# Hybrid encoder on 8 cores: two of three groups of a 31-tap depthwise convolution moved from TensorE to VectorE, and LayerNorm row sums folded before the matmul with ones

## The chip, the cores and the metric

One Trainium2 chip, 8 cores, one program on all of them; each core computes 2048 of 16384 tokens (plus a halo of up to 60 on each side), with no exchange between cores. The metric is the device time of the slowest core, in microseconds. Executions come in two states: in the slow one, the cores of a die show a lower granted TensorE clock and the time is longer (one run of the kernel before: 0.82 on one die and 0.99 on the other, 6155 us against 5217 for a fast run).

In the profiled run of the kernel before TensorE does the 33720 matmuls, VectorE (DVE, 4501 instructions) and ScalarE (ACT, 2473) the elementwise work, and GpSimd (POOL) issues the weight loads and builds 744 small diagonal matrices. The kernel keeps its tiles in a memory called SBUF; its matmuls write to the tile `bank` in PSUM.

## The reference, cut to what matters

```python
for l in range(DEPTH):                                   # DEPTH = 4, D_MODEL = 1024
    x = layer_norm(ALPHA * x + 0.5 * swiglu_ffn(x, ...ffn1...), ...)
    x = layer_norm(ALPHA * x + hybrid_mixer(x, ...), ...)
    x = layer_norm(ALPHA * x + 0.5 * swiglu_ffn(x, ...ffn2...), ...)

# in hybrid_mixer: head group C (384 channels), beside a pooling group and a short gated convolution
a = c_val * jax.nn.sigmoid(c_gate)
a = depthwise_conv(a, cconv_w) + cconv_b                 # 31 taps, one filter per channel
y_c = jax.nn.silu(layer_norm(a, cnorm_g, cnorm_b))
```

## The kernel before

Channels lie on the 128 partitions, tokens along the free dimension, so 384 channels are three groups. Each core treats its tokens in two halves; the FFN of one half runs beside the mixer of the other. A small scheduler in Python emits all instructions at build time: it estimates durations, picks what is ready and so fixes the order of every engine. **Each engine then gets its list in this fixed order**, with waits on semaphores; below, a trace shows VectorE idle for 6.1 us at an instruction that has to wait, with work behind it in its list.

The convolution is done on TensorE: for each tap POOL multiplies the identity by the tap's weights, and TensorE multiplies the shifted data by that diagonal:

```python
def diags():                                             # POOL
    for c in range(3):
        for kk in range(31):
            yield Need("pool", [], [(dgp, 1)])           # one of 4 buffers
            b = dgp.get()
            v = view2("dg", dg_t, 2, b[1], P, 0, P)
            ev = ts(v, ident_v, vcol(V_CCONV + kk * 3 + c, li), 0.0, ALU.mult, ALU.add, eng="pool")
            # ... cut ...
for c in range(3):                                       # TensorE
    for kk in range(31):
        # ... cut: wait for the diagonal ...
        for ti, (c0, n) in enumerate(tb):                # three token tiles of some 350
            me = mm_part(bk[ti][1], n, [(dv, abuf(c, c0 - base + kk - 15, n))], kk == 0, kk == 30)
        dgp.put(b, me)
    # ... cut: ACT takes the three banks out with scale 0.5 and the bias ...
```

The LayerNorm over 1024 channels sums over partitions with a matmul by a tile of ones, for each of the 8 channel chunks, once for x and once for its square:

```python
for h in range(2):                                       # two halves of 4 chunks
    # ... cut ...
    e1 = copy(cast, XS3(4 * h, 4, c0, n), rate=2.0)      # DVE, fp32 to bf16
    e2 = act(sq, XS3(4 * h, 4, c0, n), AF.Square)        # ACT
    mm_part(banks[0][1], n, [(ones_v, row_of(cast, c, n)) for c in range(4)], h == 0, h == 1)
    pe_ev = mm_part(banks[1][1], n, [(ones_v, row_of(sq, c, n)) for c in range(4)], h == 0, h == 1)
```

## Time and profile before

| | kernel before |
|---|---|
| time, three runs | 5224, 5776, 6056 us (the first in the fast state) |
| later fast runs | mostly 5217 to 5228 us |
| span of the profiled run | 5217.6 us, fast |
| TensorE busy | 5066 us, 97% |
| DVE, ACT, POOL busy | 50%, 26%, 20% |
| the chain that ended last | 95% TensorE |

One reads such a page from the chain: what lies on it is what a change can shorten. Then from the group rows: a row gives line, engine, operation, what is written from what, count, busy time, mean of one, then the engine's idle time just before these instructions and what ended it. The lines themselves stand in the prediction below.

### The profile page before, as it was taken

The page shows a single profiled execution, that of the slowest core. Times are in us where ns is not written, and L with a number is a line of the kernel's source. Part 1 is how long each engine was busy: PE and PEld are TensorE (multiplying, and loading weights), DVE is VectorE, ACT ScalarE, POOL GpSimd, SP SyncE. Part 2 cuts the span into 40 slices and gives each one's busy share as a digit, 9 for nine tenths or more (in the row PEclk, how much of TensorE's full clock was granted, in tenths as well). Part 3 has the DMA queues.
Part 4 walks back from the last instruction along what each step waited for, and adds up shares of the span by engine and source line. Part 5 has one row for each costly group of instructions (what it writes and reads, how often), then busy time and mean ns, then how long its engine had stood idle before and what let it go on. Part 6 is the DMA issues. An engine that isn't in the chain of part 4 may idle for free.

```text
span 5217.6 us, 86568 instructions; the slowest of 8 cores (5204.5 to 5217.6 us)
## 1 busy us (share of the span) xinstructions
PE 5066.0 (97%) x33720; PEld 3278.2 (63%) x33720; DVE 2634.1 (50%) x4501; ACT 1366.4 (26%) x2473; POOL 1032.9 (20%) x2050
## 2 busy tenths in 40 slices
PE   5999999999999999999999999999999999999986
PEld 2665666666666666666666666666666666666654
DVE  0354654653535555555353555655535447447534
ACT  0132232221314124122121422422212133233212
POOL 1114114111111411411111221221111141141110
PEclk8999999999999999999999999999999999999998
DMA  8543553556655355355555435435455534434663
GB/s 149 70 67 45 71 68 47 69 68 74 71 72 69 45 70 68 48 71 72 73 71 73 61 53 74 62 53 74 71 74 73 72 48 72 71 48 63 79 90 73
DMA packets 206165, 357.56 MB, mean 69 GB/s; under 512 B 21072, under 2 KB 73552, under 8 KB 205776
## 3 DMA queue, kind: packets, MB, share of 16 engines
q0 software_dynamic: 192864, 334.30, 47.9%
q1 hardware_dynamic: 12912, 17.73, 1.5%
q8 instruction: 286, 4.69, 0.4%
q14 instruction: 103, 0.84, 0.1%
HBM read 677.78 MB, written 8.39 MB: 132 GB/s over the span
## 4 chain that ended last, share of the span: by engine, by line
PE 95%; DMA 2%; POOL 1%; issue 1%; DVE 1%; ACT 0%; ACTq 0%; POOLq 0%
PE bank L460 86%; PE bank L468 9%; DMA ringF<-wgu 1%; POOL dg L510 1%; DMA xb<-xin 1%; DMA ringF<-wd 0%; DVE xs L497 0%; DVE HM L503 0%; ACT HM L490 0%; ACT xs L490 0%; DVE nw L497 0%; DVE nw L503 0%; POOL ringF L523 0%; POOL ringM L523 0%; POOL xb L523 0%
## 5 line engine op out<-in xcount | busy, mean ns | idle before, releaser
L460 PE MATMUL bank<-xb,ringF 128*128 128x352 bf16 (+7 forms) x16896 | 2560.5, 312 | 73.7 <-DMA ringF<-wgu 60.7
L460 PEld LDWEIGHTS bank<-xb,ringF 128*128 128x128 bf16 x16896 | 1642.1, 97 | 963.0 <-issue 85.8
L460 PE MATMUL bank<-HF,ringF 128*128 128x352 bf16 (+7 forms) x8448 | 1282.0, 312 | 4.0 <-DMA ringF<-wd 4.0
L503 DVE SCALAR_TENSOR_TENSOR HF<-sgF,bank 128x352 bf16<-128x352 f32 (+7 forms) x1056 | 548.4, 519 | 1389.8 <-PE bank L460 1388.4
L490 ACT ACTIVATE sgF<-bank 128x352 f32<-128x352 f32 (+7 forms) x1056 | 489.4, 463 | 2469.0 <-PE bank L460 2463.1
L460 PEld LDWEIGHTS bank<-HF,ringF 128*128 128x128 bf16 x8448 | 823.0, 97 | 442.9 <-issue 4.3
L523 POOL DMA_DIRECT2D ringF<-wgu x704 | 383.1, 544 | 2418.6 <-PE bank L460 2407.4
L460 PE MATMUL bank<-xb,ringM 128*128 128x352 bf16 (+6 forms) x3264 | 498.2, 312 | 0.0
L497 DVE TENSOR_TENSOR xs<-xs,bank 128x352 f32<-128x352 f32 (+7 forms) x624 | 324.6, 520 | 325.0 <-PE bank L460 324.9
L497 DVE TENSOR_TENSOR xs<-xs,HM 128x1408 f32<-128x1408 f32 (+7 forms) x288 | 461.8, 1611 | 0.0
L460 PEld LDWEIGHTS bank<-xb,ringM 128*128 128x128 bf16 x3264 | 316.4, 97 | 172.1 <-issue 0.2
L523 POOL DMA_DIRECT2D ringF<-wd x384 | 203.3, 529 | 998.9 <-PE bank L460 989.1
L468 PE MATMUL bank<-HM,dg 128*128 128x352 bf16 (+6 forms) x2232 | 357.5, 318 | 33.7 <-POOL dg L510 33.7
L503 DVE SCALAR_TENSOR_TENSOR xs<-xs,agb,bank 128x352 f32<-128x352 f32 (+3 forms) x336 | 192.8, 577 | 317.9 <-PE bank L460 316.3
L510 POOL TENSOR_SCALAR dg<-identf,vecs 128x128 bf16<-128x128 f32 x744 | 326.4, 442 | 57.8 <-PE bank L468 14.5
L490 ACT ACTIVATE xb<-xs,vecs 128x352 bf16<-128x352 f32 (+7 forms) x528 | 328.3, 669 | 5.8 <-DVE xs L497 5.8
L468 PEld LDWEIGHTS bank<-HM,dg 128*128 128x128 bf16 x2232 | 216.3, 99 | 172.1 <-issue 57.5
L490 ACT ACTIVATE HM<-xs 128x1408 bf16<-128x1408 f32 (+4 forms) x144 | 192.2, 1366 | 475.7 <-DVE xs L497 274.8
L503 DVE SCALAR_TENSOR_TENSOR xs<-bank,agb,xs 128x352 f32<-128x352 f32 (+3 forms) x336 | 195.4, 582 | 153.1 <-PE bank L460 153.1
L460 PE MATMUL bank<-Y,ringM 128*128 128x352 bf16 (+5 forms) x1584 | 240.8, 311 | 0.0
L460 PEld LDWEIGHTS bank<-Y,ringM 128*128 128x128 bf16 x1584 | 154.7, 98 | 79.7
L468 PE MATMUL bank<-HM,ones 128*128 128x352 bf16 (+7 forms) x1152 | 192.2, 312 | 3.3 <-DVE HM L514 1.9
(47 smaller groups left out, 1727.6 us busy)
## 6 DMA issues: line engine op xcount, KB each, us to landing
ringF<-wgu POOLq DMA_DIRECT2D x704, 256.0 KB, 5.2
ringF<-wd POOLq DMA_DIRECT2D x256, 224.0 KB, 4.1
ringM<-win POOLq DMA_DIRECT2D x136, 256.0 KB, 4.5
ringF<-wd POOLq DMA_DIRECT2D x128, 256.0 KB, 4.6
ringM<-wout POOLq DMA_DIRECT2D x64, 256.0 KB, 4.4
xs<-xin SPq DMA_DIRECT2D x3, 1488.0 KB, 29.9
out<-xs SPq DMA_DIRECT2D x3, 1408.0 KB, 5.7
xs<-xin SPq DMA_DIRECT2D x2, 1400.0 KB, 41.8
```

Of the source, the lines that this page charges most:

```text
L460: ins = e.matmul(banks_t[b][:, :n], l.ap, r.ap, start=(i == 0), stop=(i == len(prs) - 1))
L468: ins = e.matmul(banks_t[b][:, :n], l.ap, r.ap, start=start and i == 0, stop=stop and i == len(prs) - 1)
L490: return p.emit("act", lambda e: e.activation(out=out.ap, in_=in_.ap, func=func, bias=bi, scale=sc), R, [out], dur=k + size_of(out) * 0.00 ...
L497: return dve(lambda e: e.tensor_tensor(out=out.ap, in0=a.ap, in1=bap if bap is not None else b.ap, op=op), out, [a, b])
L503: return dve(lambda e: e.scalar_tensor_tensor(out=out.ap, in0=a.ap, scalar=s_, in1=bap if bap is not None else b.ap, op0=op0, op1=op1), ou ...
L510: return p.emit(eng, lambda e: e.tensor_scalar(out=out.ap, in0=a.ap, scalar1=a1, scalar2=a2, op0=op0, op1=op1), ins, [out], dur=0.15 + siz ...
L523: return p.emit(eng, lambda e: e.dma_start(out=out.ap, in_=in_.ap), R, W, dur=0.55 if eng == "pool" else 0.06, dma=sem, mbytes=mbytes)
```

## The change

Its intent: TensorE bounds the kernel and DVE is half idle, so work goes from one to the other. (1) Only channel group 2 stays on TensorE; groups 0 and 1 become 31 multiply-adds each on DVE, about 1054 tokens long, summed in fp32, at low priority in the order. (2) LayerNorm adds the chunks up in pairs on DVE before the matmuls with ones: 16 of them per token tile become 4. (3) The ring of diagonals grows from 4 to 8 and is filled earlier; the factor 0.5 moves into the taps; the durations in the scheduler are changed.

```diff
+PE_CS = [[(2,), (2,)], [(2,), (2,)], [(2,), (2,)], [(2,), (2,)]]
-            start = max(start, ev.t + (0.03 if ev.eng == eng else 0.08))
+            start = max(start, ev.t + ((0.13 if eng == "dve" else 0.03) if ev.eng == eng else 0.08))
-    dg_t = A("dg", [P, 4, P], BF16)
+    dg_t = A("dg", [P, 8, P], BF16)
 ... cut: DVE durations 0.15 + size/960 become 0.08 + size/960 ...
 ... in both hunks below the lines that only wait or hand back buffers are cut ...
+        e1 = tt(sm, XS3(0, 4, c0, n), XS3(4, 4, c0, n), ALU.add)
+        act(qa, XS3(0, 4, c0, n), AF.Square)
+        e2 = act(qb, XS3(4, 4, c0, n), AF.Square)
+        e1 = tt(half(sm, 0), half(sm, 0), half(sm, 1), ALU.add)
+        e2 = tt(qa, qa, qb, ALU.add, rate=2.0)
+        e2 = tt(half(qa, 0), half(qa, 0), half(qa, 1), ALU.add, rate=2.0)
+        mm_part(banks[0][1], n, [(ones_v, row_of(sm, c, n)) for c in range(2)], True, True)
+        pe_ev = mm_part(banks[1][1], n, [(ones_v, row_of(qa, c, n)) for c in range(2)], True, True)
 ... cut ...
+        def conv():
+            for c in [c for c in range(3) if c not in pe_cs]:
+                co = cobuf(c, 0, Wo)
+                ev = aP[c]
+                for kk in range(31):
+                    yield Need("dve", [ev], prio=1.0)
+                    av, w = abuf(c, Lo + kk - 15, Wo), vcol(V_CCONV + kk * 3 + c, li)
+                    if kk == 0:
+                        ev = ts(co, av, w, vcol(V_CB + c, li), ALU.mult, ALU.add)
+                    else:
+                        ev = stt(co, av, w, co, ALU.mult, ALU.add)
 ... cut ...
+            if c == 0:
+                S.thread(conv())
+                S.thread(diags())
-        for c in range(3):
+        for c in pe_cs:
```

More of the change, by code (lines that the diff above doesn't have):

```diff
@@ L493, in dve, with tt @@
     def dve(fn, out, ins, rate=1.0):
-        return p.emit("dve", fn, ins, [out], dur=0.15 + size_of(out) / 960.0 / rate)
-    def tt(out, a, b, op, bap=None):
+        return p.emit("dve", fn, ins, [out], dur=0.08 + size_of(out) / 960.0 / rate)
+    def tt(out, a, b, op, bap=None, rate=1.0):
         return dve(lambda e: e.tensor_tensor(out=out.ap, in0=a.ap, in1=bap if bap is not None else b.ap, op=op),
-                   out, [a, b])
+                   out, [a, b], rate)
     def stt(out, a, sc, b, op0, op1, bap=None):
@@ L510, in ts @@
         return p.emit(eng, lambda e: e.tensor_scalar(out=out.ap, in0=a.ap, scalar1=a1, scalar2=a2, op0=op0, op1=op1),
-                      ins, [out], dur=0.15 + size_of(out) / 960.0 / rate)
+                      ins, [out], dur=0.08 + size_of(out) / 960.0 / rate)
     def copy(out, a, eng="dve", rate=2.0):
         return p.emit(eng, lambda e: e.tensor_copy(out=out.ap, in_=a.ap), [a], [out],
-                      dur=0.15 + size_of(out) / 960.0 / rate)
+                      dur=0.08 + size_of(out) / 960.0 / rate)
     def memset(out, val, eng="dve"):
@@ L581, in build @@
     sgM = Pool([0, 1])
-    dgp = Pool([0, 1, 2, 3])
-    lnhalf = Pool([0, 1])
+    dgp = Pool(list(range(8)))
+    lnbuf = Pool([0, 1, 2, 3])
     rstp = Pool([0, 1])
@@ L586, in build, with ln_buf @@
     HB = 4 * NMAX * 2
-    def ln_cast(i, n):
-        return V(HMb[:, (R2 + i * 2 * HB) // 2:(R2 + i * 2 * HB) // 2 + 4 * n].rearrange("p (c t) -> p c t", c=4),
-                 mems["HM"], [(R2 + i * 2 * HB, R2 + i * 2 * HB + 8 * n)])
-    def ln_sq(i, n):
-        o = R2 + i * 2 * HB + HB
+    def ln_buf(i, n):
+        o = R2 + i * HB
         return V(HMb[:, o // 2:o // 2 + 4 * n].rearrange("p (c t) -> p c t", c=4), mems["HM"], [(o, o + 8 * n)])
@@ L653, in ln_tile, with half @@
         inv = 1.0 / D
-        yield Need("dve", [yp], [(lnhalf, 1)], cond=lambda: st["m"] == 0)
+        yield Need("dve", [yp], [(lnbuf, 3)], cond=lambda: st["m"] == 0)
         st["ln"] += 1
-        banks = None
-        pe_ev = None
-        for h in range(2):
-            if h:
-                yield Need("dve", [yp], [(lnhalf, 1)])
-            hb = lnhalf.get()
-            cast, sq = ln_cast(hb[1], n), ln_sq(hb[1], n)
-            e1 = copy(cast, XS3(4 * h, 4, c0, n), rate=2.0)
-            yield Need("act", [yp])
-            e2 = act(sq, XS3(4 * h, 4, c0, n), AF.Square)
-            yield Need("pe", [e1, e2], [(bankB, 2)] if banks is None else [], prio=-1e9)
-            if banks is None:
-                banks = (bankB.get(), bankB.get())
-            mm_part(banks[0][1], n, [(ones_v, row_of(cast, c, n)) for c in range(4)], h == 0, h == 1)
-            pe_ev = mm_part(banks[1][1], n, [(ones_v, row_of(sq, c, n)) for c in range(4)], h == 0, h == 1)
-            lnhalf.put(hb, pe_ev)
+        bufs = [lnbuf.get() for _ in range(3)]
+        sm, qa, qb = [ln_buf(b[1], n) for b in bufs]
+        def half(v, h):
+            lo = v.rng[0][0] + h * 4 * n
+            return V(v.ap[:, 2 * h:2 * h + 2, :], v.mem, [(lo, lo + 4 * n)])
+        e1 = tt(sm, XS3(0, 4, c0, n), XS3(4, 4, c0, n), ALU.add)
+        yield Need("act", [yp])
+        act(qa, XS3(0, 4, c0, n), AF.Square)
+        yield Need("act", [yp])
+        e2 = act(qb, XS3(4, 4, c0, n), AF.Square)
+        yield Need("dve", [e1])
+        e1 = tt(half(sm, 0), half(sm, 0), half(sm, 1), ALU.add)
+        yield Need("dve", [e2])
+        e2 = tt(qa, qa, qb, ALU.add, rate=2.0)
+        lnbuf.put(bufs[2], e2)
+        yield Need("dve", [e2])
+        e2 = tt(half(qa, 0), half(qa, 0), half(qa, 1), ALU.add, rate=2.0)
+        yield Need("pe", [e1, e2], [(bankB, 2)], prio=-1e9)
+        banks = (bankB.get(), bankB.get())
+        mm_part(banks[0][1], n, [(ones_v, row_of(sm, c, n)) for c in range(2)], True, True)
+        pe_ev = mm_part(banks[1][1], n, [(ones_v, row_of(qa, c, n)) for c in range(2)], True, True)
+        lnbuf.put(bufs[0], pe_ev)
+        lnbuf.put(bufs[1], pe_ev)
         yield Need("act", [pe_ev], [(rstp, 1)])
@@ L827, in mixer, with diags @@
         aP = []
+        dq = []
+        coP = [PromiseN(3) for _ in range(3)]
+        pe_cs = PE_CS[li][s]
+        def diags():
+            for c in pe_cs:
+                for kk in range(31):
+                    yield Need("pool", [], [(dgp, 1)])
+                    b = dgp.get()
+                    v = view2("dg", dg_t, 2, b[1], P, 0, P)
+                    ev = ts(v, ident_v, vcol(V_CCONV + kk * 3 + c, li), 0.0, ALU.mult, ALU.add, eng="pool")
+                    pr = PromiseN(1)
+                    pr.add(ev)
+                    dq.append((b, v, pr))
+        def conv():
+            for c in [c for c in range(3) if c not in pe_cs]:
+                co = cobuf(c, 0, Wo)
+                yield Need("dve", [], cond=lambda: len(aP) > c)
+                ev = aP[c]
+                for kk in range(31):
+                    yield Need("dve", [ev], prio=1.0)
[4 more added lines that the diff above has]
+                        ev = stt(co, av, w, co, ALU.mult, ALU.add)
+                for ti in range(3):
+                    coP[ti].add(ev)
         for c in range(3):
@@ L924, in mixer @@
         S.thread(pooling())
-        coP = [PromiseN(3) for _ in range(3)]
-        dq = []
-        def diags():
-            for c in range(3):
-                for kk in range(31):
-                    yield Need("pool", [], [(dgp, 1)])
-                    b = dgp.get()
-                    v = view2("dg", dg_t, 2, b[1], P, 0, P)
-                    ev = ts(v, ident_v, vcol(V_CCONV + kk * 3 + c, li), 0.0, ALU.mult, ALU.add, eng="pool")
-                    pr = PromiseN(1)
-                    pr.add(ev)
-                    dq.append((b, v, pr))
-        S.thread(diags())
         n_dq = 0
-        for c in range(3):
+        for c in pe_cs:
             bk = None
@@ L957, in put @@
                 def put(c=c, ti=ti, c0=c0, n=n, b=bk[ti]):
-                    ae = act(cobuf(c, c0 - Lout, n), bank(b[1], n), AF.Identity, scale=0.5, bias=vcol(V_CB + c, li))
+                    ae = act(cobuf(c, c0 - Lout, n), bank(b[1], n), AF.Identity, scale=1.0, bias=vcol(V_CB + c, li))
                     bankB.put(b, ae)
@@ L1130, in build @@
     for li in range(nl):
+        c = li * NV + V_CCONV
+        taps_v = V(vecs[:, c:c + 93], mems["vecs"], [(4 * c, 4 * c + 372)])
+        ts(taps_v, taps_v, 0.5, 0.0, ALU.mult, ALU.add)
         for w in range(3):
```

## The prediction

> **What bounds the kernel now.** The times come first. The three timed runs read 5224, 5776 and 6056 us, while the profiled run is a fast one (5219 us, cores 5204.5 to 5217.6 us, clock 0.988). I take 5224 us as the fast state and predict a fast run. Next I read the page: busy shares, the chain that ended last, and the groups.
>
> ```profile
> span 5217.6 us, 86568 instructions; the slowest of 8 cores (5204.5 to 5217.6 us)
> PE 5066.0 (97%) x33720; PEld 3278.2 (63%) x33720; DVE 2634.1 (50%) x4501; ACT 1366.4 (26%) x2473; POOL 1032.9 (20%) x2050
> ...
> PE 95%; DMA 2%; POOL 1%; issue 1%; DVE 1%; ACT 0%; ACTq 0%; POOLq 0%
> ...
> L497 DVE TENSOR_TENSOR xs<-xs,HM 128x1408 f32<-128x1408 f32 (+7 forms) x288 | 461.8, 1611 | 0.0
> ...
> L468 PE MATMUL bank<-HM,dg 128*128 128x352 bf16 (+6 forms) x2232 | 357.5, 318 | 33.7 <-POOL dg L510 33.7
> ...
> L510 POOL TENSOR_SCALAR dg<-identf,vecs 128x128 bf16<-128x128 f32 x744 | 326.4, 442 | 57.8 <-PE bank L468 14.5
> ...
> L468 PE MATMUL bank<-HM,ones 128*128 128x352 bf16 (+7 forms) x1152 | 192.2, 312 | 3.3 <-DVE HM L514 1.9
> ```
>
> TensorE bounds it: 97% busy, 95% of the chain. DVE is half idle. So each matmul removed shortens the span, unless something new makes TensorE wait. The 2232 diagonal matmuls of the 31-tap convolution hold TensorE for 357.5 us busy plus 33.7 us waiting for the diagonals that POOL builds, 391 us in all. The 1152 matmuls with ones are the LayerNorm sums. A matmul's listed 312 ns is latency: 5066/33720 is 150 ns apiece.
>
> The groups kept apart by shape give unit costs for work that goes to DVE, and all instructions on the tile dg give the spread of the diagonals:
>
> ```profile
> L503 DVE SCALAR_TENSOR_TENSOR HM<-HM,vecs 128x1054 f32<-128x1054 f32 x18 | 23.6, 1312 | 0.2
> L510 DVE TENSOR_SCALAR HM<-HM,vecs 128x1054 f32<-128x1054 f32 x9 | 6.9, 763 | 0.0
> L514 DVE CAST HM<-xs 128x1408 bf16<-128x1408 f32 x68 | 60.4, 890 | 6.5 <-PE bank L468 5.2
> L510 POOL TENSOR_SCALAR dg<-identf,vecs x744: 362/372/1424, 424.8 to 4671.8; 128x128 bf16<-128x128 f32 x186
> ```
>
> The first row is the short convolution's tap, the same instruction that the change uses 480 times. In the last, a diagonal takes 372 ns in the median but up to 1424. I looked into the first convolution stage to see when: its stretches, then the timeline of POOL, DVE and TensorE in 428 to 436 us.
>
> ```profile
> 340.00:380.00 40.00, 40.00 (x269) 25.91 (x268) 37.22 (x52) 23.06 (x44) 5.29 (x10) 1.00 0.46 60
> 360.00:425.00 65.00, 64.84 (x425) 41.16 (x423) 33.65 (x60) 39.97 (x75) 10.28 (x20) 1.00 0.50 71
> 425.00:477.00 52.00, 46.96 (x297) 28.37 (x298) 12.40 (x19) 3.22 (x7) 41.75 (x94) 1.00 0.07 11
> 428.00:436.00 8.00, 4.31 (x24) 1.71 (x21) 7.82 (x8) 0.00 (x0) 8.00 (x7) 1.00 0.00 0
> 824.00:832.00 8.00, 6.63 (x35) 3.58 (x35) 3.73 (x7) 0.00 (x0) 7.29 (x14) 0.79 0.00 0
> ```
>
> ```profile
> 427.90 8.70 POOL L510 TENSOR_SCALAR dg<-identf,vecs 128x128 bf16<-128x128 f32 x7
> 427.66 5.55 DVE L497 TENSOR_TENSOR HM<-HM 128x1100 f32<-128x1100 f32 x4
> 430.84 0.62 PE L468 MATMUL bank<-HM,dg 128*128 128x362 bf16 x3 [0.76 <-POOL dg L510]
> 432.22 0.63 PE L468 MATMUL bank<-HM,dg 128*128 128x362 bf16 x3 [0.76 <-POOL dg L510]
> ```
>
> Here lies the point of this case. While DVE runs large adds with both inputs in SBUF, back to back (5.55 us for 4), POOL makes one diagonal per DVE instruction, not one per 0.37 us: 7 in 8.70 us. TensorE then does three matmuls per 1.38 us and waits 0.76 us of it. In 824 to 832 us, during such waiting, the granted clock fell to 0.79. Before, this lasts only as long as the pooling adds.
>
> [...]the diagonals (which read the identity) are stretched to 1.4 us, while DMA issues on POOL stay at about 0.53 us in the stretch 340 to 380, where DVE is 93% busy with such adds (10 issues, 5.29 us). [...]no bf16 add exists in this trace.[...]
>
> **The change part by part.**
> (a) Convolution. Two of three channel groups leave TensorE: 2/3 of 2232 = 1488 matmuls; 248 diagonals remain, 31 in each of 8 mixers. DVE gains 8 x 2 x 31 = 496 instructions: 480 x 1.31 + 16 x 0.76 = 641 us. If the remaining diagonals come in time, a mixer needs 93 x 160 ns = 14.9 us of TensorE (357.5/2232 = 160), 119 us for eight, so 391 - 119 = 272 us are saved.
> (b) LayerNorm. Row sums are folded before the ones matmuls: 16 per tile become 4, over 72 tiles 864 fewer, x 149 ns = 129 us of TensorE. DVE loses 144 casts (128 us) and gains per tile a 1408-wide fp32 add (1.61), a bf16 add of that width[...] and two halves of that[...]: 3.2 us, 72 times, 231 us. Net +103 us.
> (c) The 0.5 of the gate moves into the taps once at the start, under 1 us; the dg ring grows from 4 to 8; diagonals are prefetched earlier. The build-time duration constants only change the static order of each engine.
> DVE total: 2634 + 641 + 103 = 3378 us, about 68% of the new span. Ideal sum: 5217.6 - 272 - 129 = 4817 us.
> (d) The new wait. The diagonals of the last group are made while DVE runs the other two groups. Between 360 and 425 us DVE has 65 - 33.65 = 31 us free, room for about 23 of 62 taps before the diagonal matmuls begin. The other 39, at 1.35 us from start to start, are 53 us of two-SBUF-input work, plus most of the stage's 12.4 us of pooling: longer than the whole matmul phase. So POOL delivers one diagonal per tap. Eight lie ready; the first refill can start after 0.45 us and lands at about 1.6 us; the 31st at 1.6 + 22 x 1.35 = 31.3 us, phase end near 31.8 instead of 14.9. TensorE cannot fill in: its order is fixed when the program is built, and before it ran the phase densely (297 matmuls in 425 to 477, 279 of them diagonal). The extra is 17 us a mixer, 136 us in eight.[...] Locked sum: 4817 + 136 + 16 = 4969 us.
>
> **Rivals.**
> R1, no lock to speak of: dg ring and early start cover it, or the taps are done sooner. For: 8 buffers. Against: they cover 8 of 31, and the DVE budget above. It gives about 4820 to 4850 us.
> R2, DVE becomes the bound of the mixer stages: taps finish late, or each 1.3 us tap delays a PSUM eviction. For: about 220 us of DVE work lie in each mixer stage of some 360 to 400 us before, and 84 us of taps go on top. Against: even that sum is below the shortened stage; in 340 to 380 DVE is 93% busy and TensorE loses nothing; evictions rank ahead of taps in the order. The first mixer's work ends near 600 us and the next FFN needs it near 700, so 100 us of slack can absorb late taps. If it fails: 5050 us or more.
> R3, slower weight loads, as POOL's queue holds locked diagonals in front of them. For: 0.07 DMA share in the diagonal phase. Against: then TensorE eats no weights either. Up to 30 us.
> The closing LayerNorm alone is DVE-bound and grows by about 4 us.
>
> **Range and chances.** I weigh the locked sum (4969) at 70%, half locked (about 4900) at 15%, R1 at 10%, R2 at 5%; with some 2 us between span and timed run, I say 4965 us. The range 4860 to 5040 us runs from half locked with some luck to locked with 70 us of small waits. Faster by over 2% means under 5120: even the locked sum is clear of it. Faster 0.94, within 2% 0.045, slower 0.015.
>
> **What would show it.** TensorE matmuls 33720 - 1488 - 864 = 31368; DVE near 3380 us busy; taps at 1.31 us. For (d): the mean of the diagonals rises from 442 ns to over 1.1 us; TensorE's wait for POOL dg rises from 33.7 us to well over 100; dips of the granted clock in all eight phases. If that wait stays under 40 us and the span is near 4830, (d) is wrong and R1 right. If waits of matmuls for DVE evictions exceed 50 us, R2 is right. DMA waits after the start over 30 us mean R3.

The locked sum of 4969 us is 4817 + 136 us and a third term of 16 us, an estimate of mine for the clock that rested on no trace; without it the sum is 4953 us. In (b) the 3.2 us a tile hold 1.6 us for the three bf16 adds; no bf16 add had been measured (the changed kernel's take 0.885 and twice 0.519 us, below). "Lock" is only a name for what the stretch 428 to 436 us shows, 1.26 us in the mean for a diagonal there against 0.37 in the median of all 744; the traces do not show what makes it.

## The result, and the profile after

The changed kernel is correct. Its fast runs read 4883 to 4918 us, most of them 4883 to 4895 (median of all 12 runs, slow ones included, 4904.7; lowest 4882.9). The ratio to the kernel before is 0.937, 95% interval 0.935 to 0.940. A ratio here is the mean time of one kernel's fast runs over that of the other's fast runs of the same rounds, so it is not quite the ratio of the medians. The medians over all runs (5529 before) are not compared: most of the runs of before were slow.

Lines of the page of the changed kernel that answer to those of before:

```profile
span 4882.7 us, 80905 instructions; the slowest of 8 cores (4870.3 to 4882.7 us)
PE 4722.2 (97%) x31368; PEld 3047.3 (62%) x31368; DVE 3298.3 (68%) x5145; ACT 1343.7 (28%) x2425; POOL 901.8 (18%) x1554
...
PE 85%; DVE 9%; issue 2%; DMA 2%; POOL 1%; ACT 0%; ACTq 0%; POOLq 0%
...
L504 DVE SCALAR_TENSOR_TENSOR HM<-HM,vecs 128x1054 f32<-128x1054 bf16 (+9 forms) x528 | 690.0, 1308 | 5.4
...
L511 POOL TENSOR_SCALAR dg<-identf,vecs 128x128 bf16<-128x128 f32 x248 | 208.0, 855 | 0.5
...
L469 PE MATMUL bank<-HM,dg 128*128 128x352 bf16 (+3 forms) x744 | 139.0, 340 | 34.4 <-POOL dg L511 34.2
```

The span fell by 335 us. TensorE is still 97% busy, with the 31368 matmuls foreseen. Taps cost 1.31 us. But the diagonals now take 855 ns in the mean, against 442 before, and their matmuls still wait 34 us, for a third of the matmuls. The matmuls' own mean went from 318 to 340 ns: part of them ran at half clock (granted 0.50 from 433.5 to 436 us, and up to 508 ns for one matmul).

From the start times of the matmuls in the trace I took each of the eight diagonal phases, from the start of the first diagonal matmul to that of the last: before 48.8 to 51.4 us (mean 50.2, 279 diagonal matmuls and 16 others in each), after 20.5 to 22.5 us (mean 21.4, 93 matmuls and nothing else). At 150 ns, 93 matmuls are 14 us. So some 7.5 us a phase, 60 us in all, are lost. The first phase of the changed kernel, as stretches of time (length, busy time of TensorE, its weight loads, DVE, ACT and POOL with counts, granted clock, share of DMA, GB/s), and DVE's longest waits within 419 to 445 us:

```profile
419.00:437.00 18.00, 14.35 (x73) 6.92 (x71) 17.16 (x23) 0.48 (x1) 16.91 (x18) 0.83 0.14 21
437.00:441.00 4.00, 4.00 (x25) 2.44 (x25) 0.00 (x0) 0.00 (x0) 2.24 (x7) 0.90 0.00 0
```

```profile
DVE xs L504 <- PE bank L461: 6.1, 1, 6.1
```

And three lines of its timeline:

```profile
429.32 0.63 PE L469 MATMUL bank<-HM,dg 128*128 128x362 bf16 x3 [0.76 <-POOL dg L511]
433.48 7.82 PE L469 MATMUL bank<-HM,dg 128*128 128x362 bf16 x36 [0.33 <-POOL dg L511]
426.15 5.55 DVE L498 TENSOR_TENSOR HM<-HM 128x1100 f32<-128x1100 f32 x4
```

For some 17 us DVE runs pooling adds and one tap, POOL gets out one diagonal per DVE instruction, and TensorE waits, as in the old kernel's pooling. Then the lock goes: from 436.6 to 442.7 us DVE does nothing. The next instruction in its fixed order is an eviction of an FFN bank whose matmuls stand in TensorE's order behind the diagonal phase. In these 6 us the diagonals come at 0.37 us each, and TensorE runs dense (36 matmuls in a row from 433.5 us on, the first 15 of them at half clock, 0.30 us apart, the last 20 at 0.155). Every phase ends with such an idle time of DVE, 4.6 to 6.8 us. The prediction had the taps run on through the whole phase. In the trace, of the 60 multiply-adds of a mixer (two further instructions are the first taps) 12 to 15 run before the phase, 1 to 3 in it and 44 or 45 behind it: what holds POOL in the phase is nearly all pooling, not taps.

The LayerNorm's groups, kept apart by shape:

```profile
L498 DVE TENSOR_TENSOR HM<-xs 128x1408 bf16<-128x1408 f32 x34 | 55.1, 1619 | 0.2
L498 DVE TENSOR_TENSOR HM<-HM 128x704 bf16<-128x704 bf16 x68 | 35.3, 519 | 0.1
L498 DVE TENSOR_TENSOR HM<-HM 128x1408 bf16<-128x1408 bf16 x34 | 30.1, 885 | 0.0
```

bf16 adds take 885 ns at 1408 elements against 1619 for the fp32 one, near half. The two bf16 widths differ by 366 ns for 704 elements, 0.52 ns each; from these, I estimate that some 150 ns of an add do not depend on its width. A tile takes 1.62 + 0.885 + 2 x 0.519 = 3.54 us, where the prediction's sum had 3.2.

### The profile page after: what moved, and what is told of

Same layout as the page of the kernel before. It is cut to its first block, busy times and chain, and to the rows that moved or that the text cites. A ratio compares the mean times of both kernels' runs of the same rounds, so it can differ in the third digit from the quotient of the medians.

```text
span 4882.7 us, 80905 instructions; the slowest of 8 cores (4870.3 to 4882.7 us)
## 1 busy us (share of the span) xinstructions
PE 4722.2 (97%) x31368; PEld 3047.3 (62%) x31368; DVE 3298.3 (68%) x5145; ACT 1343.7 (28%) x2425; POOL 901.8 (18%) x1554
## 4 chain that ended last, share of the span: by engine, by line
PE 85%; DVE 9%; issue 2%; DMA 2%; POOL 1%; ACT 0%; ACTq 0%; POOLq 0%
PE bank L461 82%; DVE HM L504 6%; PE bank L469 3%; DMA ringF<-wgu 1%; DVE xs L504 1%; POOL dg L511 1%; DMA xb<-xin 1%; DVE HF L504 1%; DVE HM L498 0%; DVE Y L498 0%; DVE xs L498 0%; DVE HM L511 0%; DMA ringF<-wd 0%; DVE HM L515 0%; ACT xs L491 0%
## 5 line engine op out<-in xcount | busy, mean ns | idle before, releaser
L524 POOL DMA_DIRECT2D ringF<-wgu x704 | 372.7, 530 | 2326.7 <-PE bank L461 2326.7
L504 DVE SCALAR_TENSOR_TENSOR HM<-HM,vecs 128x1054 f32<-128x1054 bf16 (+9 forms) x528 | 690.0, 1308 | 5.4
L491 ACT ACTIVATE HM<-xs 128x1408 bf16<-128x1408 f32 (+6 forms) x144 | 197.6, 1372 | 533.3 <-DVE xs L498 515.5
L498 DVE TENSOR_TENSOR HM<-HM 128x704 bf16<-128x704 bf16 (+25 forms) x312 | 259.3, 836 | 1.4
L511 POOL TENSOR_SCALAR dg<-identf,vecs 128x128 bf16<-128x128 f32 x248 | 208.0, 855 | 0.5
L469 PE MATMUL bank<-HM,dg 128*128 128x352 bf16 (+3 forms) x744 | 139.0, 340 | 34.4 <-POOL dg L511 34.2
```

Of the source, the lines that this page charges most:

```text
L469: ins = e.matmul(banks_t[b][:, :n], l.ap, r.ap, start=start and i == 0, stop=stop and i == len(prs) - 1)
L491: return p.emit("act", lambda e: e.activation(out=out.ap, in_=in_.ap, func=func, bias=bi, scale=sc), R, [out], dur=k + size_of(out) * 0.00 ...
L498: return dve(lambda e: e.tensor_tensor(out=out.ap, in0=a.ap, in1=bap if bap is not None else b.ap, op=op), out, [a, b], rate)
L504: return dve(lambda e: e.scalar_tensor_tensor(out=out.ap, in0=a.ap, scalar=s_, in1=bap if bap is not None else b.ap, op0=op0, op1=op1), ou ...
L511: return p.emit(eng, lambda e: e.tensor_scalar(out=out.ap, in0=a.ap, scalar1=a1, scalar2=a2, op0=op0, op1=op1), ins, [out], dur=0.08 + siz ...
L524: return p.emit(eng, lambda e: e.dma_start(out=out.ap, in_=in_.ap), R, W, dur=0.55 if eng == "pool" else 0.06, dma=sem, mbytes=mbytes)
```

## The experiments

Theory L (lock): POOL's diagonals are held while DVE executes instructions with two SBUF inputs; what is left of the loss after the change is that. Its refinement, theory F: the lock lasts as long as the two-SBUF work that DVE's fixed order holds ahead of its next wait for TensorE. Rivals: slow weight changes or the half clock itself (P), any POOL instruction suffers (W), DVE as the bound (R2). There were eleven kernels; all but one give the reference's result.

### Each part alone

The LayerNorm fold in the kernel before, nothing else:

> The kernel before with the LayerNorm fold alone; convolution untouched. Additive theory (A): 864 fewer ones matmuls at 149 ns = 129 us, so the span falls from about 5220 to about 5090 us (ratio 0.975), TensorE busy about 4937 us, and the 53 us or so that the diagonal phases lose stay lost. Rival (B): the fold makes each LayerNorm's head longer on DVE (3.2 us a tile against 1.8) and matmuls with ones wait for it, so less than 100 us come out: above 5120 us, with TensorE's waits for DVE HM grown by 30 us or more.

And the changed kernel with the old LayerNorm:

> The changed kernel with the old LayerNorm; convolution moved. Theory A: eight diagonal phases shrink from about 50 to about 21 us each, some 211 us saved beyond the FFN work in them, so about 5010 us (ratio 0.960), and the two single parts add up to the whole (129 + 211 = 340 of the measured 335). Rival B: the parts share a cost (DVE is fuller with both), so this part alone saves clearly more than 211 us, under 4990 us.

Both edits take the hunks shown above, one set each. Measured: the fold alone spans 5094 us (fast runs 5093 and 5096, ratio 0.974), the convolution alone 5010 us (5010 to 5013, ratio 0.958). From 5217.6 these are 123.5 and 207.3 us, in sum 330.8 of the measured 334.9. So the parts add up, and rival B (in the first run: waits eat the gain; in the second: the parts share a cost) is out, with one remark: in the fold, TensorE's waits for the tile HM written by DVE rose from about 2 to 11 us, all of it at the end of the program, in the last LayerNorm. By the ratio the verdict on the fold alone is unclear (interval 0.961 to 0.986, with a fast run of 5265 us among those of before); I go by the spans. DVE's busy time grew by 98.7 us with the fold (103 predicted) and by 566 with the convolution (641 predicted). Neighbouring instructions overlap in the records: the summed durations grew by 125 and 635 us. So the convolution's cost was right, and that the fold comes near 103 is in part luck.

### The diagonals on ScalarE: is it POOL?

```diff
-                    yield Need("pool", [], [(dgp, 1)])
+                    yield Need("act", [], [(dgp, 1)])
-                    ev = ts(v, ident_v, vcol(V_CCONV + kk * 3 + c, li), 0.0, ALU.mult, ALU.add, eng="pool")
+                    ev = act(v, ident_v, AF.Identity, scale=vcol(V_CCONV + kk * 3 + c, li))
```

In the changed kernel:

> The changed kernel with the diagonals built on ScalarE in place of POOL; nothing else. Lock theory (L): POOL's diagonals are held by DVE instructions with two SBUF inputs[...], the eight diagonal phases shrink from 21.3 to about 14.5 us, the wait of the matmuls for the diagonals goes from 34 us to under 5, the dips of the granted clock in the phases vanish, and the span falls by about 55 us to about 4828. Rival (P): the phases are long because a new weight tile every three matmuls, or the half clock itself, slows TensorE; then phases stay near 21 us and the time near 4885. Rival (S): ScalarE in order behind TensorE delays gates and evictions, 4885 or more.

In the kernel before:

> The kernel before with the diagonals built on ScalarE. Theory L: its diagonal phases lose 53 us to lock and clock dips (eight phases of about 50 us, of which 279 matmuls at 149 ns and 16 others make 44), so about 5170 us (ratio 0.990), with the wait for diagonals near 0. Rival P: unchanged, 5220 us. ScalarE gets 744 more instructions in these phases[...].

TensorE's and DVE's orders in the first are instruction for instruction those of the changed kernel; only POOL's and ACT's differ. The diagonals of that run, and its first phase:

```profile
L491 ACT ACTIVATE dg<-identf,vecs x248: 387/401/404, 393.2 to 4288.9; 128x128 bf16<-128x128 f32 x124
```

```profile
420.00:434.50 14.50, 14.50 (x95) 9.10 (x94) 14.15 (x20) 9.77 (x25) 0.53 (x1) 1.00 0.17 24
```

A diagonal takes 0.40 us at least, median and most, while DVE is 98% busy with the same work; TensorE is busy all of the time, the clock stays at 1.00. All eight phases take 13.1 to 14.3 us (mean 13.8 against 21.4), and no dip of the clock is left in any. The span is 4835.6 us, 47 less (fast runs 4827, 4837 and 4851, ratio 0.925). The wait of the matmuls for the diagonals has no row any more. Phases alone gave 60; the difference lies mostly behind the last phase, where TensorE waits once for weights, 16.5 us in this run (12.1 and 4.4) against 7.8. Rivals P and S are out. In the kernel before, the same edit gives 5161.5 us, 56 less (5163, 5166 and 5211, ratio 0.990 with an interval that reaches 1), its phases 44.5 to 49.1 us with more FFN matmuls in them, and no dips: the old kernel paid for the lock as well, about as much in all.

### Does it matter that POOL reads?

```diff
-                    ev = ts(v, ident_v, vcol(V_CCONV + kk * 3 + c, li), 0.0, ALU.mult, ALU.add, eng="pool")
+                    ev = memset(v, 0.01, eng="pool")
```

> The changed kernel in which POOL fills each diagonal with a constant instead of multiplying the identity: the result is wrong on purpose, TensorE's and DVE's orders are instruction for instruction the same, and POOL still writes every tile, but reads nothing from SBUF. Theory L[...]: fills stay at some 0.2 to 0.4 us beside DVE's pooling and taps, phases shrink to about 14 us, dips vanish, about 4828 us. Rival W (any POOL instruction is held while DVE works, or POOL's in-order queue is the cause): fills stretched to about 1.4 us, phases near 21 us, 4885 us.

```profile
L519 POOL MEMSET dg<- x248: 194/204/682, 396.5 to 4293.7; 128x128 bf16 x124
```

The result is wrong, as intended (relative error 0.14). The fills take 204 ns in the median beside the same DVE work, phases are 13.1 to 14.3 us, the span 4839.1 us. So beside DVE's pooling and multiply-adds it is not POOL, nor its queue, nor its writes that matter: it is POOL's read. Rival W is out.

The trace also shows which DVE instructions hold a reading POOL. In the changed kernel 121 diagonals start beside a long DVE instruction with two SBUF inputs: 1368 ns in the median. Another 22 start beside one that reads PSUM: 362 or 363 ns. But 7 start beside a first tap of the convolution (`tensor_scalar`, one SBUF input) and take 678 to 913 ns, so two inputs are not the whole rule. The first tap clashes with fills that only write as well. Two fills that started during one took 653 and 682 ns and ended 0.14 us after it. In five other places eight fills went through at 223 ns each, and the tap took 1.92 to 2.10 us, where it takes 0.81 to 0.83 us with the diagonals on ScalarE:

```profile
746.73 1.92 DVE L511 TENSOR_SCALAR HM<-HM,vecs 128x1054 f32<-128x1054 bf16 x1
746.85 1.24 POOL L519 MEMSET dg<- 128x128 bf16 x8
```

These first taps lie outside the diagonal phases (sixteen in the program), so the account of the phases stands.

### How long does the lock last?

One build-time constant: the scheduler believes that a diagonal matmul takes 2.2 times as long. Nothing is added; DVE's order gets 14 to 16 taps behind the pooling, ahead of the eviction on which it would wait, where it had 1 to 3. TensorE's order in the phase stays (93 diagonal matmuls in a row), but outside the phases it changes too.

```diff
-                    me = mm_part(bk[ti][1], n, [(dv, abuf(c, c0 - base + kk - 15, n))], kk == 0, kk == 30)
+                    me = mm_part(bk[ti][1], n, [(dv, abuf(c, c0 - base + kk - 15, n))], kk == 0, kk == 30, slow=2.2)
```

> The changed kernel with one build-time constant altered: the schedule is told that a diagonal matmul takes 2.2 times as long. No instruction is added or dropped and TensorE's 93 diagonal matmuls stay dense; but DVE's static order now has 14 more taps in a row behind the pooling, ahead of the eviction that waits for TensorE. Theory F (the lock lasts as long as the two-SBUF work that DVE's order puts ahead of its next wait for TensorE): phases grow from 21.3 to about 31 us, the diagonals' mean from 0.86 to about 1.2 us, and the time by about 80 us to about 4965, the locked sum of the prediction. Rival G (POOL gets through by itself after a while, whatever DVE does, or the phase is limited by something else): phases stay near 21 us, time near 4885.

```profile
L511 POOL TENSOR_SCALAR dg<-identf,vecs x248: 362/1358/1498, 394.7 to 4426.7; 128x128 bf16<-128x128 f32 x124
```

```profile
419.00:447.00 28.00, 19.23 (x95) 8.72 (x93) 27.30 (x31) 0.67 (x2) 26.42 (x24) 0.87 0.07 12
```

Now DVE is busy for the whole phase, the median diagonal is a held one (1358 ns; 673 in the changed kernel), and phases take 26.2 to 29.0 us (mean 27.5). In the trace, of the 23 diagonals made in a phase 17 to 19 took over 1 us, against 10 to 12 in the changed kernel. The span is 4977 us (fast runs 4979, 4980, 4994, ratio 0.952), 95 us more. Theory F holds and G is out, though not every size: the phases grew by 6 us, not 10, and account for 49 of the 95 us. Of the other 46, 24 are lost in the 200 matmuls right behind the phases, and about 11 behind the last phase, where one wait for weights is 10 us longer. That evictions queueing behind taps cause the 24 us is likely (TensorE's waits for DVE grew by 16 us) but not shown, since TensorE's order differs there.

The other side of the same model: the scheduler is told that POOL needs 1.38 us for a diagonal (its `ts` gets `dur=1.38`), so that TensorE's order has FFN groups within the phase.

> The changed kernel with another build-time constant altered: the schedule is told that a diagonal on POOL takes 1.38 us. TensorE's order then has four to six groups of eight FFN matmuls inside each diagonal phase. Theory F: the waits are filled with that work, so the 60 us lost to gaps in the phases halve: about 4850 us, clock dips fewer. If DVE instead gets more taps into the longer phase and the fill is too small, the time stays between 4870 and 4900.

This missed. TensorE's order did get 24 to 32 other matmuls into each phase. But the scheduler gave DVE taps for the longer phase too: the two-SBUF work in a phase rose from 16 to 18 us to 27 to 30 us (9 to 12 taps in it, where there were 1 to 3), the median diagonal to 1331 ns, and phases to 30.1 us in the mean. Behind them TensorE waited for DVE:

```profile
PE bank L461 <- DVE HM L498: 23.0, 15, 3.9
```

In the changed kernel there is no such row for this line. The span is 4974.9 us, 92 worse (fast runs 4976, 5005 and 5007 us, ratio 0.954). Filling a wait was no help here, since the same step fed what causes it. I did not try to change TensorE's order alone.

### How large a ring?

> The changed kernel with 4 diagonal buffers in place of 8; TensorE's and DVE's orders are the same. Theory F: some 16 us of two-SBUF work in a phase let about 12 diagonals through; with 4 in stock instead of 8, four more groups of matmuls (0.45 us each) come after the lock: 1.8 us a phase, about 14 us in all, 4890 to 4905 us. Rival N (each group that was not in stock costs a whole wait of 0.9 us): 29 us, 4912 us or more. Rival M (ring size is irrelevant): 4885 us.

The edit is `Pool(list(range(4)))` in place of `range(8)`; TensorE's and DVE's orders are the same. Span 4900.8 us (fast runs 4901 and 4903, ratio 0.937), 18 us more; phases 21.7 to 24.3 us (mean 23.1 against 21.4: 1.7 us a phase), with the same 10 to 12 held diagonals in each. Theory F's 1.8 us a phase is met (14 of the 18 us lie in the phases); the ratios alone could not tell these two kernels apart, the spans and the phases do.

### More and fewer groups on TensorE

```diff
-PE_CS = [[(2,), (2,)], [(2,), (2,)], [(2,), (2,)], [(2,), (2,)]]
+PE_CS = [[(1, 2), (1, 2)]] * 4          # the second run: [[(), ()]] * 4
```

Two groups on TensorE:

> The changed kernel with two of three groups on TensorE. Theory F: the phase is 186 matmuls, 28 us dense, and the order can put up to 28 us of pooling and taps beside it, so about 20 diagonals come at 1.35 us and the rest at the free rate: phases of 38 to 45 us, 130 to 190 us more than the changed kernel's 171 in all, so 5010 to 5070 us. If a phase lost a fixed 6.5 us whatever its length (theory K): 34.5 us, 4990 us.

Phases of 43.7 to 48.3 us, the span 5100 us on two cores and 5060 to 5071 on the other six (fast runs 5069 to 5102, ratio 0.971). A fixed loss per phase (theory K) would give 34.5 us: out. In each phase 22 of the 54 diagonals made are held for over 1 us, against 10 to 12 of 23 with one group; phases and time are a little above the range that theory F gave.

No group on TensorE, hence no diagonals and no lock:

> The changed kernel with all three convolution groups on DVE, no diagonals at all. If TensorE stays the bound (theory T): the eight phases of 21.3 us go, 171 us, so about 4712 us; DVE busy about 3298 + 8 x 31 x 1.31 = 3623 us, 77%. If DVE becomes the bound of the mixer stages (R2 of the prediction): in a stage of some 330 us lie about 220 + 126 us of DVE work, so the mixers finish after the FFN that runs beside them and TensorE waits some 10 to 40 us in each of eight: 4790 to 5000 us.

```profile
PE bank L469 <- DVE HM L504: 152.0, 27, 9.0
PE bank L469 <- DVE HM L498: 81.3, 32, 4.8
...
PE bank L461 <- ACT xb L491: 66.0, 19, 7.5
```

5101.6 us (fast runs 5100 to 5103, ratio 0.974), 219 us worse than with one group (against the kernel before unclear, interval 0.963 to 0.985). Here R2 of the prediction comes true: DVE, 70% busy in the mean, is 90% busy from 640 to 1000 us, where TensorE does 315 us of work in 360; TensorE waits 152 and 81 us with its ones matmuls for DVE and 66 us for the normalised input. In 640 to 700 us of this run TensorE is busy for 32 of 60 us and the clock is granted at 0.72.

### The durations alone, and the best kernel once more

> The kernel before with the new build-time duration constants of DVE alone: same instructions, another static order. The prediction took this to be neutral: 5215 to 5230 us, TensorE's waits for POOL dg near 34 us. If the constants carried part of the gain: under 5200 us.

5221.7 us (fast runs 5223 and 5224, ratio 0.998): neutral, as the prediction took it, with TensorE's waits for POOL dg at 30.2 us.

> The changed kernel with the diagonals on ScalarE once more, in five rounds, for a firm ratio: about 4830 us in fast runs, ratio to the kernel before 0.925, against 0.937 of the changed kernel, every phase near 14 us.

Of six runs only two were fast, 4848.0 and 4847.8 us, so no interval is given; their mean over that of the four fast runs of before (5234.7) is 0.926. Phases 13.1 to 14.3 us again. The 4830 us expected were not met. All five fast runs of this kernel lie in 4827 to 4851 us: it beats both kernels, the changed one by 47 us in the profiled span of the first run (4835.6 and 4882.7) and 36 in the second (4846.5).

## Why the prediction was right or wrong, point by point

- **What bounds the kernel, and the ideal sum (4817 us): right.** With the lock taken away the span was 4835.6; of the 18 us above, TensorE's waits for DVE there (10.9, 4.5 and 2.0 us, against 2.1 in the kernel before) explain most. Part (b), 129 us: TensorE's busy time fell by 129.2 with the fold alone, the span by 123.5, and the waits at the closing LayerNorm rose by 9 us (the prediction said about 4). Parts are additive.
- **The mechanism of (d), the lock: right,** and beside the pooling and the multiply-adds it is POOL's read: diagonals on ACT (0.40 us) or filled without reading (0.20 us) free the phases. The reading of the stretch 340 to 380 us went a little far: two-SBUF instructions are 29 of DVE's 37 us there, not all.
- **The size of (d): wrong, and this is the term that makes 4965 us some 80 us too high.** The step was that 39 taps, right behind the pooling, would let POOL deliver one diagonal per tap to the end, a phase of 31.8 us, 17 us lost in each. Measured: 1 to 3 taps in a phase and 44 or 45 behind it, phases of 21.4 us, 7.5 lost, because only 10 to 12 of the 23 refills were held, nearly all by the pooling. So taps added little to the lock; the old kernel had lost about as much to its pooling (56 us by the run with its diagonals on ScalarE). I had used that TensorE's order is fixed at build time and forgot that DVE's is too: the scheduler, which believed the phase to last about 14 us, put only about that much work ahead of the next eviction, and then DVE stood still for 6 us behind an eviction that TensorE had yet to feed. The run with 14 to 16 taps in that place gave 4977 us, near the 4969 that the prediction called the locked sum; that nearness is partly luck, as half of its extra lies outside the phases. My weight of 70% should have gone to what I had called half locked (15%), for which the prediction had no mechanism.
- **The signs.** Mean of the diagonals "over 1.1 us": 0.855. The wait for POOL dg "well over 100 us": 34.2, no more than before. That row is a poor gauge: 60 us are lost by start times. The clock stood at half for 41 us of the phases, where dense matmuls start 0.30 us apart and not 0.155, so that less of the delay shows as a gap. It stood there for 3.4 or 6.8 us in each of seven phases. In the first of them four gaps of 0.64 to 0.76 us, about one every 1.4 us, came before; but between 427 and 435 us of the kernel before six gaps of 0.41 to 0.77 us left the clock at 1.00, so when it falls is not shown. "Dips in all eight": in seven, but six of the eight phases had one in the kernel before (27 us at half clock), so this sign told little.
- **R1** (no lock to speak of) was wrong, **R2** false for this change (TensorE's waits for DVE: 16 us) and true one group further, **R3** unseen: weight waits after the start came to 7.8 us (13.1 before).
- The change forecast for fast runs was -5.0% (4965 over 5224); measured -6.3%. The fast runs, 4883 to 4918 us, lie in the lower part of the range of 4860 to 5040.

## What to carry to other kernels

When work goes to VectorE, look at what GpSimd does at that time: here VectorE instructions of about 1000 elements with two SBUF inputs stretched a GpSimd instruction that reads SBUF from 0.37 to 1.37 us, and moving this small producer to ScalarE gave 47 us for two lines. Where orders are fixed at build time, follow the chain through every engine's order: here it was VectorE's own stall that let GpSimd, and with it TensorE, catch up. And shift work only until the receiving engine is full in the stage concerned, not on the average: one group less on TensorE gained, the last one cost 219 us.
